# Two fp32 layers on one core: four small re-orderings around the adaLN sums, the gate products, v's transposes and the attention's denominators

## The chip, the cores and the metric

The kernel runs on one core of one Trainium2 chip. The metric is the device time of one execution in microseconds (us), lower is better. Engines: TensorE (PE; its weight loads are listed as PEld), VectorE (DVE), ScalarE (ACT), GpSimd (POOL) and SyncE (SP), whose queue starts most of the loads.

## The reference

A backbone of two layers over 256 latent and 256 context tokens, 1024 features, in float32:

```python
def modulate(x, shift, scale):
    return x * (1 + scale) + shift
def adaln(cvec, w, b):
    return jnp.split(jax.nn.silu(cvec) @ w + b, 6, axis=-1)
...
# every sub-layer: x <- LN(ALPHA*x + gate * F(x*(1+scale)+shift))
# layer 0: F = Conformer convolution module, then a squared-ReLU MLP
# layer 1: F = bidirectional chunkwise mLSTM (4 heads of 512, inner 2048), then the MLP
def sq_relu_mlp(u, w1, w2):
    return jnp.square(jax.nn.relu(u @ w1)) @ w2
...
q, k, v = xc @ w_q, xc @ w_k, xm @ w_v
gates = jnp.concatenate([q, k, v], axis=-1) @ w_gate + b_gate
...
den = jnp.sum(scores, axis=-1) + w_inter * jnp.einsum('bhtd,bhd->bht', qc, n)
h = num / jnp.maximum(jnp.abs(den), jnp.exp(-m_row))[..., None]
```

## The kernel before

Activations lie with features on the 128 partitions and tokens along the free axis; the two streams (latent, context) lie side by side, 512 columns. Every float32 operand is split into a rounded high part and a low part (`split`: ACT casts `wh`, DVE subtracts to get `wl`), and each product is three matmuls (`mm3`, L175, L178, L179; `mm3t`, L206 to L208, for products with the transposed result). Weights come in 1 MB loads (`raw_load`, L148, on SP's queue) into three buffers `raw`, and are split into four buffers `wh` and four `wl`. PSUM is shared by four kinds of bank: `mm` three, `ln` two, `cv` two, `fl` one.

The program is written in the order of its work, with generators that advance side work by one step between the pieces of a large product. The framework's scheduler sets each engine's order from the order of the program and from the semaphores that it needs; `issue_after(x)` asks that what is inside be put behind instruction x, and `lastmm[0]` is the newest large matmul. Each engine then runs its instructions in that order.

The places that the change touches:

- `AdaV` makes one adaLN vector on DVE beside a large product. `step()` loads a 256 KB piece of `ada_w` and adds it, times c, into accumulators (the tiles S and L). When a vector's pieces are through, two closures go onto the list `todo` and are run one at each later step: `sums` (four matmuls with a column of ones over the partitions, L431, and a copy into F on ACT, L433) and `end` (four transposes of F, L440, and an addition on DVE). `flush()` runs what is left. Three vectors are made: in the first MLP, in its second part, and in the mLSTM's products. The second is `ada_n1`, whose flush is in `feed0`, when the layer-norm of the first MLP is closed for the high half of the tokens. The first MLP's last product, w2 of part 3, goes over the high half of the tokens first and then the low half (`gemm2`); the epilogue L1043 adds each output to the residual x out of a `mm` bank, and the normalisation (L567, L568), the scaling (L590, ACT) and the subtraction (L591) of the high half run beside the low half's matmuls.
- `wgq_step` folds the gate's weights through wq, so that the gates can be had from the input: it loads a 1 MB piece of `wqT` and multiplies it with a 128x32 piece of the gate's weights, four matmuls of 512 columns at four column positions (L748), adding up in one `fl` bank over sixteen pieces. Behind the sixteenth, ACT copies the bank into F (L753) and four transposes (L756) turn it. `v_epi` ends each of the sixteen output tiles of v; `v_out` transposes the tile (L1193) and stores it, a tile later, through the list `late` and `flush()`. The loop over `gemm_steps(wv, ...)` (32 steps of 24 large matmuls) calls `wgq_step` in each of its first 16 steps and a step of the third AdaV in the other 16.
- `weights(h)` makes the attention's weights of head h: scores, exponentials, and on GpSimd (L1454) the sum `es` over the blocks. Two empty yields behind, it makes the denominators: `es` times a column of ones (L1461), Abs on ACT (L1463), two maxima with the guard and a reciprocal on DVE, in `rden[h]`. `attend(h)` makes the four outputs (direction by token block) in two `cv` banks, and DVE scales each by `rden` (L1533). ACT also runs the sigmoid of `gate_o` (L1500) and the exponentials (L1442) in that stretch, with a table load at each change between them. Generators of two heads run beside one another.

Of the kernel before, what the change touches and what calls it, by code (L numbers as in the profile page):

```python
# [14 lines left out]
P = 128  # L15
# [3 lines left out]
ET = E // P  # L19
# [51 lines left out]
def hybrid_kernel(ctx: ExitStack, tc: tile.TileContext, xT, vecs_d, wdw_d, ada0_w, ada_w, wg_d, pw1a, pw1, pw2, w1_0, w2_0,  # L71
                  w1_1, w2_1, up_x, up_z, wv, wo, bo_d, wk, wq, wqT, wdown, rows_d, out):
    nc = tc.nc
# [26 lines left out]
    def psum(tag="mm"):  # L100
        return pp.tile([P, 512], F32, tag=tag, name=nm(tag), bufs={"mm": 3, "ln": 2, "fl": 1, "cv": 2}[tag])
# [23 lines left out]
    ident = con.tile([P, P], F32, name="ident")  # L125
# [55 lines left out]
    lastmm = [None]  # L181
# [22 lines left out]
    def mm3t(ps, xh, xl, wh, wl, start, stop):  # L204

        nc.tensor.matmul(ps, xh, wh, start=start, stop=False)  # L206
        nc.tensor.matmul(ps, xl, wh, start=False, stop=False)  # L207
        nc.tensor.matmul(ps, xh, wl, start=False, stop=stop)  # L208
# [181 lines left out]
    class AdaV:  # L390
# [8 lines left out]
        def step(self):  # L399
            if self.todo:  # L400
                self.todo.pop(0)()
            n, kt = divmod(self.i, DT)
            if n == len(self.units):
                return
            if kt == 0:
                self.acc += [tmp("SL"[(len(self.acc) + i) // 2 % 2]) for i in range(len(self.streams))]
            w = adp.tile([P, 512], F32, tag="ar", name=nm("ar"))
            nc.sync.dma_start(w, ada_w[self.l, self.units[n], kt // 4, :, kt % 4 * 512:kt % 4 * 512 + 512])
            for i, s in enumerate(self.streams):
                a, c = self.acc[i - len(self.streams)], cs[:, kt, 14 + s:15 + s]  # L410
                if kt == 0:
                    o = nc.vector.tensor_scalar(a, w, c, None, op0=ALU.mult)
                    if i == 0:
                        tc.keep_in_program_order(o)
                else:
                    nc.vector.scalar_tensor_tensor(a, w, c, a, op0=ALU.mult, op1=ALU.add)  # L416
            self.i += 1
            if kt == DT - 1 and n < self.ncol and len(self.acc) == 4:
                accs, self.acc = self.acc, []
                u = self.units[n] + 1 - 4 // len(self.streams)  # L420
                self.todo += [lambda: self.sums(accs), lambda: self.end(u)]

        def flush(self):
            while self.todo:
                self.todo.pop(0)()
# [9 lines left out]
        def end(self, u):  # L435
            ns, s0 = len(self.streams), self.streams[0]
            nu, o = 4 // ns, _OFF[f"ada_b{self.l}"][0] + 4 * u
            tr = psum()
            for b in range(4):
                nc.tensor.transpose(tr[:, b * P:(b + 1) * P], self.sb[:, b * P:(b + 1) * P], ident)  # L440
            nc.vector.tensor_tensor(
                ada[self.l][:, 4 * u:4 * (u + nu), s0:s0 + ns].rearrange("p (v b) s -> p b v s", b=4),
                tr.rearrange("p (b v s r) -> p b v s r", b=4, v=nu, s=ns)[:, :, :, :, 0],
                vecs[:, o:o + 4 * nu].rearrange("p (v b o) -> p b v o", b=4, o=1).broadcast_to([P, 4, nu, ns]), op=ALU.add)
# [295 lines left out]
    def wgq_step():  # L740
        kt = len(wqs)
        if kt == 0:
            wqs.append(psum("fl"))
        else:
            wqs.append(None)
        raw = raw_load(wqT[kt])
        for j in range(4):
            nc.tensor.matmul(wqs[0][32 * j:32 * j + 32, :], wgp[0][:, kt, :], raw[:, j * 512:(j + 1) * 512],  # L748
                             start=kt == 0, stop=kt == ET - 1, tile_position=(0, 32 * j))
        if kt < ET - 1:  # L750
            return
        qsb = tmp("F")
        nc.scalar.copy(qsb, wqs[0])  # L753
        qtr = psum("fl")
        for b in range(4):
            nc.tensor.transpose(qtr[:, b * P:(b + 1) * P], qsb[:, b * P:(b + 1) * P], ident)  # L756
        nc.vector.tensor_copy(wgp[1].rearrange("p (j b) c -> p j b c", j=4)[:, :, :, 0:16],
                              qtr.rearrange("p (b j c) -> p j b c", b=4, j=4)[:, :, :, 0:16])
# [421 lines left out]
    def v_epi(m, ps):  # L1180
        vt = B("vt").rearrange("p a b -> p (a b)")[:, :T]
        nc.scalar.copy(vt, ps)
        vts.append(vt)
        flush()
        late.append(lambda: v_out(m, vt))

    def v_out(m, vt):
# [27 lines left out]
    vstep = 0  # L1215
    for _ in gemm_steps(wv, range(8), xm, T, v_epi):
        vstep += 1
        if vstep <= ET:
            wgq_step()
        else:  # L1220
            ada_n2.step()
        if vstep in (20, 26):
            xc_load(0 if vstep == 20 else 4)
# [196 lines left out]
    def weights(h):  # L1420


        es = ES()
        short = PW(F32R)
        for d in range(2):
            cidx = gcol(d, h)
            nb = psum("ln")
            nc.tensor.matmul(nb[:, :C], sel[d * 4 + h], negm, start=True, stop=True)
            yield
            for i, b in enumerate(blocks[d]):  # L1430
                q0, q1 = rng[d, b]
                if i != 1:
                    et = tmp("S")
                e_ = et[:, HI] if i == 1 else et[:, q0:q1]
                if b < 2:
                    nc.scalar.activation(e_, nb[:, q0:q1], AF.Exp, bias=acol[:, b, cidx:cidx + 1])
                else:
                    mk = mask[:, d, :, :].rearrange("p a t -> p (a t)")
                    off = {(0, 2): 0, (0, 3): 0, (1, 3): 0, (1, 2): P}[d, b]
                    nc.vector.scalar_tensor_tensor(e_, nb[:, q0:q1], acol[:, b, cidx:cidx + 1],  # L1440
                                                   mk[:, off:off + q1 - q0], op0=ALU.add, op1=ALU.add)
                    nc.scalar.activation(e_, e_, AF.Exp)  # L1442
                nc.vector.tensor_tensor(e_, e_, S[h, b][:, q0:q1], op=ALU.mult)
                if q1 - q0 == C:
                    t = PW(F32R)
                    hi, lo = t[:, LO], t[:, HI]
                else:
                    hi, lo = short[:, 2 * d * P:(2 * d + 1) * P], short[:, (2 * d + 1) * P:(2 * d + 2) * P]
                split(hi, lo, e_)
                pw[h, d, b] = (hi, lo)  # L1450
                if i == 1:
                    nc.gpsimd.tensor_tensor(es[:, d, :], et[:, LO], et[:, HI], op=ALU.add)
                elif i > 1:
                    nc.gpsimd.tensor_tensor(es[:, d, q0:q1], es[:, d, q0:q1], e_, op=ALU.add)  # L1454
                yield
        yield
        yield
        den = psum("ln")
        for d in range(2):
            for t in range(2):  # L1460
                nc.tensor.matmul(den[:, 2 * d + t:2 * d + t + 1], es[:, d, BLK[t]], ones[:, 0:1], start=True, stop=True)  # L1461
        rden[h] = rd = con.tile([P, 2, 2], F32, name=nm("rden"))
        nc.scalar.activation(rd, den[:, 0:4].rearrange("p (d t) -> p d t", d=2), AF.Abs)  # L1463
        for d in range(2):
            cidx = gcol(d, h)
            nc.vector.tensor_tensor(rd[:, d, :], rd[:, d, :], guard[:, :, cidx:cidx + 1].rearrange("p t o -> p (t o)"),
                                    op=ALU.max)
        nc.vector.reciprocal(rd, rd)


    xls = []
    for i in range(2):
        rx = raw_load(xl_dr[i].rearrange("p b c -> p (b c)"))
        for j in range(8):
            t = XL(F32R)
            split(t[:, LO], t[:, HI], rx[:, j * C:(j + 1) * C])
            xls.append((t[:, LO], t[:, HI]))
    og, yy, rden = {}, {}, {}

    def gate_o(h):  # L1480

# [32 lines left out]
    def attend(h):  # L1514
# [8 lines left out]
        for t in range(2):  # L1523
            for d in range(2):
                ps = psum("cv")
                bl = [b for b in blocks[d] if rng[d, b][0] <= t * P < rng[d, b][1]]
                for i, b in enumerate(bl):
                    hi, lo = pw[h, d, b]
                    sl = slice(t * P - rng[d, b][0], t * P - rng[d, b][0] + P)
                    vh, vl = [v_[:, (b % 2) * DH:(b % 2 + 1) * DH] for v_ in vs[b // 2]]  # L1530
                    mm3t(ps, hi[:, sl], lo[:, sl], vh, vl, i == 0, i == len(bl) - 1)
                o_ = og[h, d, t]
                nc.vector.scalar_tensor_tensor(o_, ps, rden[h][:, d, t:t + 1], o_, op0=ALU.mult, op1=ALU.mult)  # L1533
                yield
            hj = og[h, 0, t]
            nc.vector.tensor_tensor(hj, hj, og[h, 1, t], op=ALU.add)
            nc.vector.bn_stats(st_[:, t, :], hj)
            nc.vector.bn_aggr(mv[:, t, 0:2], st_[:, t, :])
            hs.append(hj)
            yield  # L1540
# [346 lines left out]
```

## Time and profile before

| what | value |
| --- | --- |
| three runs | median 1698.73 us (1697.41 to 1699.22) |
| the profiled execution | 1699.18 us; its span 1697.5 us |
| granted TensorE clock | 0.998 |
| instructions | 22796 |
| PE busy | 1669.2 us (98% of the span) |
| DVE, ACT, POOL busy | 1033.0, 744.0, 44.3 us |
| chain that ended last | PE 92%, DVE 5%, ACT 1%, DMA 1% |
| moved by DMA | 300.54 MB, 177 GB/s over the span |

In a row of the timeline stand start and duration in us, engine, line, operation, out<-in and the number of instructions joined (xcount); in square brackets the idle time of the engine ahead of it and what released it. A matmul's duration overlaps the next one's, so its cost is read from the starts. In the lists of waits stand total, times and longest, in us.

### The profile page before, as it was taken

Reading aid. Unit: us, or ns where it says so; the run is one execution under the profiler, and the core shown is the slowest. Engines: PE = TensorE matmul, PEld = TensorE weight load, DVE = VectorE, ACT = ScalarE, POOL = GpSimd, SP = SyncE. Lnnn points to the kernel's source line nnn. Section 1 sums busy time; section 2 is a strip of 40 time slices with the busy share of each in tenths; the row PEclk is TensorE's granted clock in tenths of the full one; section 3 lists DMA queues with packets and bytes.
Section 4 is the critical chain, followed back from the end, with each engine's and each line's share of the span. In section 5 each row is a group of like instructions: output and inputs, shape, how many; then the busy total and the mean of one; then the engine's idle time right before and its main releaser. Section 6 shows DMA issues by size and latency. Waiting matters only on the chain.

```text
span 1697.5 us, 22796 instructions
## 1 busy us (share of the span) xinstructions
PE 1669.2 (98%) x8878; PEld 1363.8 (80%) x8878; DVE 1033.0 (61%) x1841; ACT 744.0 (44%) x1195; POOL 44.3 (3%) x92
## 2 busy tenths in 40 slices
PE   7999999999999999999999999999999999999997
PEld 5655898878888998876788899888877878878886
DVE  5555795666645776751243653563487786776676
ACT  3312563232324476642333533442477564645443
POOL 0000000000000000000000000000011120000001
PEclk9999999999999999999999999999999999999999
DMA  8546322434424065567765752454454556756552
GB/s 340 198 156 243 111 75 95 157 128 146 145 100 148 2 211 180 183 238 252 251 214 174 251 181 105 155 189 171 157 190 176 193 195 209 257 211 229 192 184 89
DMA packets 70828, 300.54 MB, mean 177 GB/s; under 512 B 7170, under 2 KB 22018, under 8 KB 40384
## 3 DMA queue, kind: packets, MB, share of 16 engines
q1 hardware_dynamic: 53056, 284.39, 47.6%
q10 hardware_dynamic: 17664, 14.69, 2.7%
q8 instruction: 70, 1.15, 0.3%
q14 instruction: 38, 0.31, 0.1%
HBM read 283.32 MB, written 15.73 MB: 176 GB/s over the span
## 4 chain that ended last, share of the span: by engine, by line
PE 92%; DVE 5%; ACT 1%; issue 1%; DMA 1%; POOL 0%; SPq 0%; DVEq 0%; POOLq 0%; ACTq 0%
PE mm L175 17%; PE mm L178 17%; PE mm L179 17%; PE mm L190 7%; PE mm L191 4%; PE mm L206 3%; PE mm L207 3%; PE mm L208 3%; PE cv L208 2%; PE cv L207 2%; PE cv L206 2%; PE fl L335 1%; DVE wl L153 1%; PE fl L748 1%; PE cv L830 1%
## 5 line engine op out<-in xcount | busy, mean ns | idle before, releaser
L153 DVE TENSOR_TENSOR wl<-raw,wh 128x1024 fp32r<-128x1024 f32 x346 | 424.7, 1233 | 275.8 <-ACT wh L152 271.4
L152 ACT CAST wh<-raw 128x1024 fp32r<-128x1024 f32 x346 | 360.6, 1050 | 494.5 <-PE mm L178 269.0
L178 PE MATMUL mm<-u,wh 128*128 128x512 f32 (+1 forms) x808 | 292.9, 363 | 0.1
L175 PE MATMUL mm<-u,wh 128*128 128x512 f32 (+1 forms) x680 | 245.5, 361 | 0.2 <-ACT E L770 0.2
L179 PE MATMUL mm<-u,wl 128*128 128x512 f32 (+1 forms) x680 | 242.3, 357 | 0.0
L178 PEld LDWEIGHTS mm<-u,wh 128*128 128x128 f32 x808 | 153.4, 190 | 23.5 <-issue 1.8
L175 PEld LDWEIGHTS mm<-u,wh 128*128 128x128 f32 x680 | 129.2, 190 | 28.8 <-issue 9.1
L179 PEld LDWEIGHTS mm<-u,wl 128*128 128x128 f32 x680 | 129.2, 190 | 18.4 <-issue 0.2
L175 PE MATMUL mm<-xm,wh 128*128 128x512 f32 x256 | 102.2, 399 | 0.0
L206 PE MATMUL mm<-wh,xl 128*128 128x512 f32 x256 | 101.3, 396 | 0.5 <-ACT wh L152 0.5
L207 PE MATMUL mm<-wh,xl 128*128 128x512 f32 x256 | 100.9, 394 | 0.0
L179 PE MATMUL mm<-xm,wl 128*128 128x512 f32 x256 | 99.9, 390 | 0.0
L208 PE MATMUL mm<-wl,xl 128*128 128x512 f32 x256 | 99.6, 392 | 0.0
L175 PE MATMUL mm<-hid,wh 128*128 128x512 f32 (+1 forms) x256 | 93.1, 364 | 0.0
L178 PE MATMUL mm<-hid,wh 128*128 128x512 f32 (+1 forms) x256 | 92.8, 363 | 0.0
L179 PE MATMUL mm<-hid,wl 128*128 128x512 f32 (+1 forms) x256 | 92.7, 362 | 0.0
L190 PE MATMUL mm<-x,wh 128*128 128x512 f32 x232 | 81.0, 398 | 0.8 <-DVE x L1698 0.8
L416 DVE SCALAR_TENSOR_TENSOR S<-ar,cs,S 128x512 f32<-128x512 f32 x56 | 40.8, 749 | 61.3 <-DMA ar<-ada_w 61.0
L178 PE MATMUL mm<-qq,wh 128*128 128x272 f32 x256 | 73.9, 289 | 0.0
L175 PE MATMUL mm<-qq,wh 128*128 128x272 f32 x256 | 73.5, 289 | 0.0
L179 PE MATMUL mm<-qq,wl 128*128 128x272 f32 x256 | 73.5, 288 | 0.0
L190 PE MATMUL mm<-u,wh 128*128 128x512 f32 x192 | 68.6, 399 | 0.0
(507 smaller groups left out, 3277.8 us busy)
## 6 DMA issues: line engine op xcount, KB each, us to landing
raw<-w SPq DMA_DIRECT2D x64, 1024.0 KB, 4.8
raw<-wo SPq DMA_DIRECT2D x32, 1024.0 KB, 4.9
raw<-ada_w SPq DMA_DIRECT2D x26, 1024.0 KB, 5.9
ar<-ada_w SPq DMA_DIRECT2D x80, 256.0 KB, 3.4
raw<-wv SPq DMA_DIRECT2D x16, 1024.0 KB, 5.4
raw<-wqT SPq DMA_DIRECT2D x16, 1024.0 KB, 5.6
raw<-wq SPq DMA_DIRECT2D x16, 1024.0 KB, 4.9
raw<-wk SPq DMA_DIRECT2D x16, 1024.0 KB, 5.2
```

The costliest lines, as they stand in the source:

```text
L152: c = nc.scalar.copy(hi, src)
L153: nc.vector.tensor_tensor(lo, src, hi.bitcast(F32), op=ALU.subtract)
L175: a = nc.tensor.matmul(ps, wh, xh, start=start, stop=False)
L178: nc.tensor.matmul(ps, wh, xl, start=False, stop=False)
L179: lastmm[0] = nc.tensor.matmul(ps, wl, xh, start=False, stop=stop).ins
L190: todo = [lambda s_, e_: nc.tensor.matmul(ps, wh, r[0], start=s_, stop=e_), lambda s_, e_: nc.tensor.matmul(ps[:, :n], wl, r[0][:, :n], st ...
L191: lambda s_, e_: nc.tensor.matmul(ps[:, :n], wl, r[0][:, :n], start=s_, stop=e_)]
L206: nc.tensor.matmul(ps, xh, wh, start=start, stop=False)
L207: nc.tensor.matmul(ps, xl, wh, start=False, stop=False)
L208: nc.tensor.matmul(ps, xh, wl, start=False, stop=stop)
L335: a = nc.tensor.matmul(ps[32 * j:32 * j + 32], cs[:, kt, 14 - 2 * v:46 - 2 * v], blocks[kt], start=first and kt < 4, stop=last and kt >= 4 ...
L416: nc.vector.scalar_tensor_tensor(a, w, c, a, op0=ALU.mult, op1=ALU.add)
```

## The change

Four edits. The denominators move out of `weights(h)` into a function of their own, called in `attend(h)` behind the matmuls of the head's first output; odd heads sum `es` in the tile F. An AdaV's `sums` and `end` get an empty step between them, and the end's transposes are issued behind the newest large matmul. Two products of wq stand together at the odd steps 3 to 17 of v's product; the AdaV steps stay where they were. v's finished tiles are transposed two at a time.

```diff
@@ AdaV.step
-                self.todo += [lambda: self.sums(accs), lambda: self.end(u)]
+                self.todo += [lambda: self.sums(accs), lambda: None, lambda: self.end(u)]
@@ AdaV.end
             tr = psum()
-            for b in range(4):
-                nc.tensor.transpose(tr[:, b * P:(b + 1) * P], self.sb[:, b * P:(b + 1) * P], ident)
+            with tc.issue_after(lastmm[0]):
+                for b in range(4):
+                    nc.tensor.transpose(tr[:, b * P:(b + 1) * P], self.sb[:, b * P:(b + 1) * P], ident)
@@ v_epi
         vts.append(vt)
-        flush()
+        if m % 2 == 0:
+            flush()
         late.append(lambda: v_out(m, vt))
@@ loop over gemm_steps(wv, ...)
         vstep += 1
-        if vstep <= ET:
+        if vstep % 2 and 3 <= vstep <= ET + 1:
             wgq_step()
-        else:
+            wgq_step()
+        if vstep > ET:
             ada_n2.step()
@@ weights(h)
-        es = ES()
+        es = tmp("F").rearrange("p (d t) -> p d t", d=2) if h % 2 else ES()
...
-        yield
-        yield
-        den = psum("ln")
+        sums[h] = es
+
+    def denominators(h):
+
+        den, es = psum("ln"), sums[h]
         for d in range(2):
             for t in range(2):
                 nc.tensor.matmul(den[:, 2 * d + t:2 * d + t + 1], es[:, d, BLK[t]], ones[:, 0:1], start=True, stop=True)
...
@@ attend(h), behind an output's matmuls
                     mm3t(ps, hi[:, sl], lo[:, sl], vh, vl, i == 0, i == len(bl) - 1)
+                if h not in rden:
+                    denominators(h)
                 o_ = og[h, d, t]
```

Lines after the change are one higher from L421 on, three to six higher in the last third.

On PE in v's product, before: one tile's transposes and one product, two steps (48 large matmuls) from the next transposes; `fl` is the bank of the products.

```order
L179 MATMUL mm_7189<-xm_6683,wl_7307 128x512
L1193 MATMUL ln_7336<-ident,vt_7290 128x128 x4
L748 MATMUL fl_6737<-raw_7344,wgq_556 32x512 x4
L175 MATMUL mm_7358<-xm_5920,wh_7362 128x512
L178 MATMUL mm_7358<-u_5921,wh_7362 128x512
```

The same place after, at the last pair of products; L757 is the transposing of the folded gate weights.

```order
L179 MATMUL mm_7330<-xm_6275,wl_7335 128x512
L749 MATMUL fl_6797<-raw_7362,wgq_556 32x512 x4
L749 MATMUL fl_6797<-raw_7368,wgq_556 32x512 x4
L175 MATMUL mm_7331<-xm_5920,wh_7386 128x512
L178 MATMUL mm_7331<-u_5921,wh_7386 128x512
L179 MATMUL mm_7331<-xm_5920,wl_7387 128x512
L175 MATMUL mm_7331<-xm_5969,wh_7386 128x512
L757 MATMUL fl_7376<-ident,F_7374 128x128 x4
```

Two products stand directly behind one another; the transposes that need ACT's copy F stand four large matmuls behind them, where there were twelve.

On DVE at the close of the first MLP, before: x_119 to x_417 are features of the high half in normalisation, `mm_5000` the low half's second output.

```order
L556 TENSOR_TENSOR L_4896<-ident,lc_4893 128x512
L567 TENSOR_TENSOR x_119<-x_119,ln_4898 128x256
L568 TENSOR_TENSOR x_119<-x_119,ln_4898 128x256
L567 TENSOR_TENSOR x_153<-x_153,ln_4898 128x256
L1043 SCALAR_TENSOR_TENSOR x_325<-mm_5000,ada_105,x_325 128x256
L568 TENSOR_TENSOR x_153<-x_153,ln_4898 128x256
```

The same place after, the end of the normalisation; ahead of it stand now the addition of `ada_106` and the six operations that make the columns `ca` and `cb`.

```order
L569 TENSOR_TENSOR x_371<-x_371,ln_4892 128x256
L568 TENSOR_TENSOR x_417<-x_417,ln_4892 128x256
L592 TENSOR_TENSOR u_4951<-S_4952,u_4950 128x256
L569 TENSOR_TENSOR x_417<-x_417,ln_4892 128x256
L1044 SCALAR_TENSOR_TENSOR x_325<-mm_5000,ada_105,x_325 128x256
L592 TENSOR_TENSOR u_4959<-S_4960,u_4958 128x256
```

The emptying of the bank `mm_5000` moved from behind the third normalisation operation to behind the sixteenth.

On PE in head 0's attention, before: the denominators among the products of `gate_o`.

```order
L207 MATMUL mm_11047<-wh_11135,xl_10760 128x512
L1461 MATMUL ln_11083<-ones,es_10911 128x1
L208 MATMUL mm_11047<-wl_11136,xl_10760 128x512
L1461 MATMUL ln_11083<-ones,es_10911 128x1
L206 MATMUL mm_11048<-wh_11135,xl_10757 128x512
```

After: one block behind the first output, `cv_11301`; `cv_11322` is the second, `cv_11373` the third.

```order
L208 MATMUL cv_11301<-wl_11280,pw_10949 128x512
L1466 MATMUL ln_11311<-ones,es_10911 128x1 x4
L206 MATMUL cv_11322<-wh_11275,pw_10999 128x512
L207 MATMUL cv_11322<-wh_11275,pw_10999 128x512
L208 MATMUL cv_11322<-wl_11276,pw_10999 128x512
```

The block stands 16 large matmuls ahead of the third output's first one.

More of the change, by code (lines that the diff above doesn't have):

```diff
@@ L1477, in hybrid_kernel @@
             xls.append((t[:, LO], t[:, HI]))
-    og, yy, rden = {}, {}, {}
+    og, yy, rden, sums = {}, {}, {}, {}
     def gate_o(h):
```

## The prediction

> **What bounds the kernel now.** I read the page's head, its engine table and the shares of the chain first, then the waits of PE, then the timeline of PE at each place that the diff touches.
>
> ```profile
> span 1697.5 us, 22796 instructions
> PE 1669.2 (98%) x8878; PEld 1363.8 (80%) x8878; DVE 1033.0 (61%) x1841; ACT 744.0 (44%) x1195; POOL 44.3 (3%) x92
> PE 92%; DVE 5%; ACT 1%; issue 1%; DMA 1%; POOL 0%; SPq 0%; DVEq 0%; POOLq 0%; ACTq 0%
> ```
>
> The tensor engine is busy for 98% of the span and is 92% of the chain that ended last. So an edit counts in full where it shortens PE's own stream or one of PE's waits; what it does to DVE, ACT or the queues counts only when PE then stands still. The large matmuls are untouched, and what can be won is what lies between them. From the waits of PE (total, times, longest, in us), the three lines that the change touches:
>
> ```profile
> PE ln L1461 <- POOL es L1454: 1.6, 3, 0.9
> PE mm L440 <- ACT F L433: 0.8, 1, 0.8
> PE mm L206 <- ACT wh L152: 0.5, 1, 0.5
> ```
>
> That is 2.9 us in all, 0.2% of the span. The rest of a possible gain is the price of interrupting the stream of 128x512 matmuls. About 0.2% (3.4 us) is what a measurement of this kernel can tell from no change.
>
> **Part 1, the products of wq two by two.** Sixteen products of wgq (8 matmul records each) stand alone in the stream today. The timeline of PE around one of them (start, duration, instruction):
>
> ```profile
> 736.73 0.39 PE L179 MATMUL mm<-xm,wl 128*128 128x512 f32 x1
> 737.05 1.06 PE L748 MATMUL fl<-raw,wgq 128*32 128x512 f32 x8
> 738.05 0.50 PE L175 MATMUL mm<-xm,wh 128*128 128x512 f32 x1
> 738.38 0.39 PE L178 MATMUL mm<-u,wh 128*128 128x512 f32 x1
> 738.62 0.39 PE L179 MATMUL mm<-xm,wl 128*128 128x512 f32 x1
> ```
>
> The large matmuls start 0.23 us apart (738.38 to 738.62 here; 0.227 on a long stretch). From 736.73 to 738.62 are three such steps, 0.68 us; it took 1.89. The product costs 1.21 us: 1.00 from its start to the next matmul, the rest in going in and out of the stream. The changed kernel issues 16 records in one piece, eight times. No such piece of wgq is in the trace, but the same form with 16 records is, in the third adaLN vector:
>
> ```profile
> 1529.37 0.39 PE L190 MATMUL mm<-x,wh 128*128 128x512 f32 x1
> 1529.69 1.92 PE L335 MATMUL fl<-raw,cs 128*32 128x512 f32 x16
> 1531.55 0.50 PE L206 MATMUL ln<-wh,hid 128*128 128x512 f32 x1
> 1531.89 0.40 PE L207 MATMUL ln<-wh,hid 128*128 128x512 f32 x1
> 1532.13 0.40 PE L208 MATMUL ln<-wl,hid 128*128 128x512 f32 x1
> ```
>
> From 1529.37 to 1532.13 are 2.76 us, less 0.68 is 2.08. Two single products cost 2.42, a double one 2.08: 0.34 saved, eight times, **-2.7 us**. Bounds: nothing saved, and 0.68 saved each (the second product entering for the 0.8 us by which eight more records lengthen the row and no more), so 0 to -5.4. I take the middle because it is measured on the same form.
>
> What hangs on it: each pair needs two 1 MB loads of wqT at once, and their two buffers become free only behind the pair. That is a rival below. The transposes behind the last product wait for one ACT copy with 4 matmuls (0.9 us) for cover where there were 12; the copy itself lasts 0.6, so I cost that at 0, and at up to 1 us if ACT is in the middle of a cast.
>
> **Part 2, v's transposes two tiles at once.** Sixteen blocks of four:
>
> ```profile
> L1193 PE MATMUL ln<-ident,vt 128*128 128x128 f32 x64 | 9.8, 276 | 0.0
> ```
>
> In the new order four of the eight pairs of blocks stand directly behind one another and four have 4 large matmuls between them, because the second transposes wait for the second copy. If a merged block saves the same share as a wgq pair, 0.34 of 2.42 (14%), then of the four blocks' worth, at most 9.8 us / 16 = 0.61 each, it is 4 x 2 x 0.61 x 0.14 = 0.7; but going out and in is less than that for short blocks. I take **-0.2 us**, 0 to -0.7.
>
> **Part 3, adaLN sums a step apart.** The timeline of PE at the first vector's end, and the row of the second's:
>
> ```profile
> 376.68 0.39 PE L179 MATMUL mm<-hid,wl 128*128 128x512 f32 x1
> 377.45 0.60 PE L431 MATMUL mm<-S,ones 128*32 128x512 f32 x2
> 378.82 0.66 PE L440 MATMUL mm<-ident,F 128*128 128x128 f32 x4 [0.76 <-ACT F L433]
> 379.23 0.48 PE L175 MATMUL mm<-hid,wh 128*128 128x512 f32 x1
> 511.14 0.60 PE L440 MATMUL mm<-ident,F 128*128 128x128 f32 x4
> ```
>
> From 376.99 on the four sums run, ACT copies them, and the four transposes stand directly behind and wait 0.76 us. With an empty step between and the transposes issued behind the newest large matmul, 25 rows lie between: the wait goes, **-0.7 us**. The second end (511.14) and the third wait for nothing now, so there is nothing to gain there.
>
> The second one is moved to a worse place. Its vector has 32 steps and 34 calls; the empty step pushes the end past the last call, into the flush when the last layer-norm of the high half is closed. Then its transposes stand behind the last output of that half, and on DVE one addition and six small operations that make the scale and shift columns stand inside the normalisation. The rows of that place, from the timelines of DVE, ACT and PE:
>
> ```profile
> 575.28 0.42 DVE L567 TENSOR_TENSOR x<-x,ln 128x256 f32<-128x256 f32 x1 [1.28 <-PE ln L561]
> 576.47 0.48 DVE L1043 SCALAR_TENSOR_TENSOR x<-mm,ada,x 128x256 f32<-128x256 f32 x1
> 576.19 0.60 ACT L590 ACTIVATE u<-x,cb,ca 128x256 fp32r<-128x256 f32 x1 [3.57 <-DVE x L568]
> 577.32 0.60 ACT L590 ACTIVATE u<-x,cb,ca 128x256 fp32r<-128x256 f32 x1
> 582.03 0.28 PE L175 MATMUL mm<-hid,wh 128*128 128x256 f32 x1
> ```
>
> The operation at 576.47 empties the PSUM bank of the low half's second output, and the fifth output, which begins on PE at 582.03, writes that bank. Today it stands behind three normalisation operations and is 5 us early. In the new order it stands behind all sixteen and six subtractions. The subtractions wait for ACT's pairs of scalings, 1.13 us apart (576.19 to 577.32). With the transposes (0.47 us) and the seven operations ahead, I put the first scaling at about 576.8; the sixth pair ends near 576.8 + 6 x 1.13 = 583.6, the subtraction and the normalisation behind it and the bank's operation (0.42 + 0.42 + 0.48, overlapping a little) end near 584.6. PE, later by the transposes, wants the bank at 582.5. Cost **+2.0 us**. Bounds: if DVE and ACT run as tightly as 0.34 us an operation, +0.5; if they run at DVE's present mixed pace of 25 us for 61 operations (0.41), 22 x 0.41 = 9.0 from 575.9, +2.9 with the bank's operation:
>
> ```profile
> 575.00:600.00 25.00, 25.00 (x208) 24.81 (x207) 23.68 (x61) 15.93 (x29) 0.00 (x0) 1.00 0.12 43
> ```
>
> **Part 4, the denominators.** Today 32 short matmuls (16 pairs in ones, twos and fours) are spread over the gaps and can come before GpSimd has finished the sums es. Behind the change they come in four blocks of eight records, behind the head's first output, long after es.
>
> ```profile
> L1461 PE MATMUL ln<-ones,es 128*128 128x1 f32 x32 | 4.6, 240 | 1.7 <-POOL es L1454 1.6
> 1285.97 0.39 PE L206 MATMUL mm<-wh,xl 128*128 128x512 f32 x1
> 1286.95 0.60 PE L1461 MATMUL ln<-ones,es 128*128 128x1 f32 x4 [0.60 <-POOL es L1454]
> ```
>
> The number of matmuls is the same, so their own time stays. What goes is the waits: from 1285.97 to 1286.95 is 0.98 where 0.23 is the pace, so 0.75 lost where the list prints 0.60; the 1.6 us of the list are 2.0 by that ratio. With the 0.5 of the wait for a cast behind the last denominator (ACT's queue had held the cast behind its wait), it is -2.5.
>
> That odd heads sum into the tile F costs nothing: its last user before them is the third adaLN vector's end, a stage before the heads.
>
> New is that the first output's scaling, and behind it the third output (two cv banks), waits for Abs on ACT, two maxima and a reciprocal on DVE. In head 0, ACT reloads its tables at that time:
>
> ```profile
> 1283.02 1.28 ACT L1442 ACT_TABLE_LOAD   x1
> 1284.32 0.31 ACT L1442 ACTIVATE S<-S 128x128 f32<-128x128 f32 x1
> L1533 DVE SCALAR_TENSOR_TENSOR og<-cv,rden,og x16: 736/750/751, 1280.7 to 1472.2; 128x512 f32<-128x512 f32 x16
> L1463 ACT ACTIVATE rden<-ln x4: 173/174/174, 1270.1 to 1385.6; 128x4 f32<-128x4 f32 x4
> ```
>
> ACT leaves its last table load and exponential at 1284.6; Abs, 0.17, stands behind them, then two maxima of 0.15, the reciprocal of 0.17 and the scaling of 0.75, 1.4 us, with some 0.1 for each hand-over: 1286.4. The end of the first output is near 1282.1 in today's time, some 0.8 earlier without the blocks that stood ahead of it; the third output begins 0.9 (the new block) and 16 matmuls (3.6) later, 1285.8. That is +0.6 there; a cast of the next weights stands behind Abs too and is wanted 4 matmuls earlier. Heads 1 and 2 have room (24 matmuls and more, no table load), head 3 perhaps 0.1. New wait **+0.7**, bounds 0 and +2. Together **-1.8 us**, bounds -2.9 and -0.5.
>
> [...]
>
> **The sum.** -2.7 - 0.2 - 0.7 + 2.0 - 1.8 = -3.4 us. The profiled execution took 1699.18 us (span 1697.5 and 1.7 around it), so 1695.8 by its time; the median of the three runs, 1698.73, is 0.45 lower, which gives **1695.3 us**. It is a forecast of many small terms whose largest two have opposite signs.
>
> **The rivals.**
>
> *The merges bring nothing.* If the cost of a product is its 8 records and not the way in and out, -2.7 and -0.2 fall to about -0.3. Against it stands the 16-record row with 2.08; for it, that this row is followed by another kind of matmul (wh stationary), which may hide some. Then 1695.8 + 2.6 - 0.45 = 1697.9: within 0.2%.
>
> *The flush and the denominators cost more.* If the bank's wait takes its upper bound, +2.9, and head 0's wait +2, the sum is -3.4 + 0.9 + 1.3 = -1.2: 1697.5, within 0.2% as well. What speaks for it: DVE is already 95% busy in those 25 us (23.68 of 25.00).
>
> *Slower: the pairs wait for their loads.* The stage's loads, from the DMA view and the waits of SP's queue, 730 to 850 us:
>
> ```profile
> DMA packets 9462, 30.54 MB, mean 254 GB/s; under 512 B 759, under 2 KB 5321, under 8 KB 6345
> raw<-wqT SPq DMA_DIRECT2D x14, 1024.0 KB, 5.4
> raw<-wv SPq DMA_DIRECT2D x10, 1024.0 KB, 5.4
> SPq L148 <- PE fl L748: 77.5, 15, 7.8
> ```
>
> Three buffers hold raw weights. Today one load of wqT is asked for every 6.7 us; behind the change two are asked for together, when the pair is through, and the next pair is 48 x 0.227 = 10.9 us behind its end. In that time two loads of wqT and one of wv, 3.15 MB, have to land. At the mean rate of 254 GB/s they take 12.4 us, 1.5 too many; that is where it decides: above 3.15 MB / 10.9 us = 289 GB/s nothing waits. Seven pairs have a pair ahead of them: 7 x 1.5 = 10.5 us, so 1695.3 + 10.5 = 1705.8, slower. What speaks against it: 77.5 us of SP's time went on waiting for the products to free a buffer, so the mean rate is what was asked for and not what the memory gives; two loads of 5.4 us one behind the other take 10.8, and wv's is split into its halves well ahead of use. [...]
>
> *It doesn't do what it says.* The order of PE's rows shows every one of the four edits made, so this has no chance of its own.
>
> **How the numbers follow.** Forecast 0.58, merges without gain 0.12, flush and denominators dearer 0.14, loads late 0.10; 0.06 is left for a larger gain than I see (up to -5.4 for the pairs, -2.9 for the denominators: 1691). The forecast's own range is 1692.5 to 1698, from its terms' bounds taken two at a time. The range for 8 in 10 is 1691.5 to 1700.5: it holds the two cases near 1697.5 and some of a small lateness of loads, and leaves out the full one. "Faster by over 0.2%" begins at 1695.3, the middle of the forecast: 0.29 of its 0.58, 0.06 of the larger gain, and the forecast's tail towards a cheaper flush, which I hold for somewhat likelier than a dearer one because 2.0 was taken with ACT's whole pace, 0.08: **0.43**. Slower by over 0.2% is 0.10 for the loads and 0.04 for two mishaps at once: **0.14**. The rest, **0.43**, is within 0.2%.
>
> **What would show it.** Right: 16-record rows of wgq with about 2.1 us from the matmul ahead to the third behind, and no idle time noted beside them; no wait of L441 for F; no wait of ones,es; one idle time of 1.5 to 2.5 us near 584 us on PE, released by DVE x. Wrong: idle time beside raw<-wqT from DMA (the loads); a wait of cv on DVE og over 1.5 us (denominators); PE running through 582 to 585 without a gap (the flush costs nothing, and the total is near 1693); a double product at 2.4.

## The result and the profile after

The changed kernel takes 1695.8 us (median of 20 runs, 1692.83 to 1698.71), the kernel before 1698.25 (20 runs beside them): ratio 0.9985, 95% interval 0.9979 to 0.9990, 2.5 us less. In a second set of 12 runs it was 1694.61 against 1698.45, ratio 0.9977 (0.9967 to 0.9987). One run of the kernel before took 4330 us and is left out of all figures. The gain is real: 0.15% in the first set, inside the 0.2% that the prediction took for no change, and 0.23% in the second. The first median is 0.5 us from the forecast (1695.3). But the runs of the changed kernel lie 6 to 8 us apart, and the experiments had to say why.

The head of the page and the waits of PE after the change (total, times, longest, in us):

```profile
span 1695.9 us, 22802 instructions
PE 1668.2 (98%) x8878; PEld 1367.8 (81%) x8878; DVE 1031.1 (61%) x1841; ACT 743.0 (44%) x1195; POOL 44.3 (3%) x92
PE mm L175 <- DVE x L1044: 1.1, 1, 1.1
PE fl L206 <- DVE E L1604: 1.0, 2, 0.6
PE mm L208 <- DVE wl L153: 0.6, 1, 0.6
```

All three waits of PE that the prediction listed (for es, for F, for a cast) are gone. Three others stand in their place, 2.7 us in all where it was 2.9. The gain is in PE's stream and not in its waits. From the timeline of PE, a pair of products, whose cost is read as before, from the start of the matmul ahead to the third behind:

```profile
747.38 0.39 PE L179 MATMUL mm<-xm,wl 128*128 128x512 f32 x1
747.69 1.92 PE L749 MATMUL fl<-raw,wgq 128*32 128x512 f32 x16
749.55 0.50 PE L175 MATMUL mm<-xm,wh 128*128 128x512 f32 x1
749.89 0.40 PE L178 MATMUL mm<-u,wh 128*128 128x512 f32 x1
750.13 0.40 PE L179 MATMUL mm<-xm,wl 128*128 128x512 f32 x1
```

From 747.38 to 750.13 are 2.75 us, less three steps of 0.227 is 2.07; the row of the same form in the trace of before had given 2.08. Then the flush, first DVE (start of the normalisation, and the emptying of the bank), then PE:

```profile
573.69 0.42 DVE L568 TENSOR_TENSOR x<-x,ln 128x256 f32<-128x256 f32 x1 [1.28 <-PE ln L562]
581.39 0.47 DVE L1044 SCALAR_TENSOR_TENSOR x<-mm,ada,x 128x256 f32<-128x256 f32 x1
```

```profile
580.56 0.28 PE L179 MATMUL mm<-hid,u 128*128 128x256 f32 x1
581.92 0.39 PE L175 MATMUL mm<-hid,wh 128*128 128x256 f32 x1 [1.08 <-DVE x L1044]
```

PE stops ahead of the matmul that the prediction named, for 1.24 us more than the usual step of 0.12; the sign named beforehand was 1.5 to 2.5. And one thing that no part of the change explains: PE at half pace, at the start of the attention.

```profile
1247.05 0.70 PE L1431 MATMUL ln<-negm,ident 36*128 36x256 f32 x2
1247.68 0.63 PE L208 MATMUL mm<-wl,xl 128*128 128x512 f32 x1
1248.11 0.63 PE L206 MATMUL mm<-wh,xl 128*128 128x512 f32 x1
...
1250.67 0.63 PE L206 MATMUL mm<-wh,xl 128*128 128x512 f32 x1
1251.42 0.39 PE L208 MATMUL mm<-wl,xl 128*128 128x512 f32 x1
```

The matmuls start 0.43 us apart for 3.4 us and then 0.23 again, which costs some 1.3 to 1.6 us here (table below). It happens once more from 1503.89 to 1507.30. The profiled run of before has neither of these two stretches, but it has one at 170 us, and so have six others of the twelve profiled runs (e8 has it at 108). The granted clock (the figure behind the last count in brackets) of these stretches, first before, then after:

```profile
170.24:173.65 3.41, 3.41 (x17) 3.19 (x16) 1.19 (x3) 3.13 (x9) 0.00 (x0) 0.50 0.70 293
```

```profile
1247.90:1251.30 3.40, 3.40 (x9) 2.61 (x9) 1.45 (x4) 3.37 (x7) 0.73 (x1) 0.50 0.88 281
1503.89:1507.29 3.40, 3.40 (x11) 2.92 (x12) 3.36 (x15) 3.40 (x11) 0.00 (x0) 0.50 0.99 407
```

To keep such things apart, I compare six stretches of each profiled run with the same stretches of before. The marks are starts on PE: the first adaLN sums, the first transposes behind the first MLP (128x128 into cv), the last product cv<-vt,wgv, the transposes of negm ahead of the attention, the second transposes of res behind it, and the end of the span. In the trace of before they are at 376.99, 642.65, 937.55, 1248.71, 1500.66 and 1697.5 us. Differences to before in us; "h" marks a half-pace stretch in the columns "attention" and "tail".

| kernel | to the first sums | MLP | v | to the attention | attention | tail | span |
| --- | --- | --- | --- | --- | --- | --- | --- |
| changed kernel | -0.65 | +0.43 | -2.80 | -0.02 | +0.03 h | +1.41 h | -1.6 |
| the same again (e10) | +0.26 | +0.41 | -2.74 | -0.22 | -0.12 h | +1.41 h | -1.0 |
| pairs alone (e1) | -1.93 | 0.00 | -2.54 | +0.19 | -0.13 | +0.21 | -4.2 |
| adaLN alone (e2) | -1.83 | +0.40 | -0.01 | 0.00 | +1.40 h | -0.06 | -0.1 |
| denominators alone (e3) | -1.72 | -0.03 | +0.01 | -0.19 | -1.55 | -0.02 | -3.5 |
| end before the flush (e4) | -1.54 | -0.74 | -2.43 | -0.06 | -1.49 | -0.04 | -6.3 |
| the same again (e8) | +0.32 | -0.75 | -2.61 | -0.16 | -0.15 h | +1.35 h | -2.0 |
| e4, v one by one (e6) | -0.99 | -0.73 | -2.53 | -0.12 | +0.11 h | +1.36 h | -2.9 |
| e4, three products (e5) | -1.77 | -0.73 | +7.58 | -0.13 | -1.68 | +0.13 | +3.4 |
| e4, gap filled, ten (e7) | -0.44 | -0.74 | -2.98 | -0.12 | -1.65 | +0.73 | -5.2 |
| e4, gap filled, five (e9) | -0.28 | -0.74 | -2.97 | +0.20 | -1.68 | -0.03 | -5.5 |

The first column is the same work in every kernel, and it differs by 2.3 us between runs: single spans are not to be compared, stretches are. An early half-pace stretch (at 170 or 108 us) is probably part of it: the four runs without one (e1, e2, e4, e6) are among the six shortest there, and the six longest all have one.

### The profile page after: what moved, and what is told of

Same layout as the page of the kernel before. It is cut to its first block, busy times and chain, and to the rows that moved or that the text cites. A ratio compares the mean times of both kernels' runs of the same rounds, so it can differ in the third digit from the quotient of the medians.

```text
span 1695.9 us, 22802 instructions
## 1 busy us (share of the span) xinstructions
PE 1668.2 (98%) x8878; PEld 1367.8 (81%) x8878; DVE 1031.1 (61%) x1841; ACT 743.0 (44%) x1195; POOL 44.3 (3%) x92
## 5 line engine op out<-in xcount | busy, mean ns | idle before, releaser
L175 PE MATMUL mm<-u,wh 128*128 128x512 f32 (+1 forms) x680 | 244.7, 360 | 0.3 <-ACT E L771 0.3
L175 PEld LDWEIGHTS mm<-u,wh 128*128 128x128 f32 x680 | 129.2, 190 | 28.7 <-issue 9.1
L175 PE MATMUL mm<-xm,wh 128*128 128x512 f32 x256 | 101.0, 395 | 0.0
L175 PE MATMUL mm<-hid,wh 128*128 128x512 f32 (+1 forms) x256 | 93.3, 364 | 1.1 <-DVE x L1044 1.1
L175 PE MATMUL mm<-qq,wh 128*128 128x272 f32 x256 | 73.5, 288 | 0.0
## 6 DMA issues: line engine op xcount, KB each, us to landing
ar<-ada_w SPq DMA_DIRECT2D x80, 256.0 KB, 3.4
```

The costliest lines, as they stand in the source:

```text
L175: a = nc.tensor.matmul(ps, wh, xh, start=start, stop=False)
```

## The experiments

### e1: only the pairs

The edit is the loop over `gemm_steps(wv, ...)` of the change and nothing else.

> Only the products of wq two by two, all else as before. Theory (each pair saves the way in and out of the stream once, 0.34 us): pieces of 16 records with 2.09 us each instead of two of 1.22, so 8 x 0.34 = 2.7 us less at equal clock, 1698.3 to about 1695.6; no idle time beside the loads of wqT. Rival (a pair's two loads are late): idle time on PE from DMA raw<-wqT ahead of some pairs, and less than 2 us saved.

Measured: 1697.08 us (11 runs), ratio 0.9994 (0.9985 to 1.0003), which can't be told from no change. The stage of v is 2.54 us shorter, with pieces of 16 records at 2.08 to 2.09 and no wait for a load. So the theory holds for the stage, and the total shows only half of it; the runs reach from 1694.5 to 1699.4.

### e2: only the adaLN edit

The edit is the empty step in `step` and the `issue_after` in `end`.

> Only the adaLN sums a step apart and the end's transposes behind the newest large matmul. Theory: the wait of 0.76 at the first end goes (-0.74), and the second end in the flush brings one idle time of about 1.1 to 1.3 us on PE near 583 us, released by DVE's emptying of a bank; together +0.3 to +0.6 us. Rival (the stop near 583 comes from the changed phase of other edits, not from this one): no idle time there, and 0.7 us less than before.

Measured: 1699.49 us (11 runs), ratio 1.0010 (1.0001 to 1.0019): a little slower. From the timeline of PE:

```profile
579.36 0.28 PE L179 MATMUL mm<-hid,u 128*128 128x256 f32 x1
580.72 0.38 PE L175 MATMUL mm<-hid,wh 128*128 128x256 f32 x1 [1.08 <-DVE x L1044]
```

The stop comes with this edit alone. The MLP's stretch is 0.40 longer: -0.73 up to the second sums, +1.13 behind them. This run also has a half-pace stretch near 1249 us, with the attention as it was before the change.

### e3: only the denominators

The edit moves them out of `weights` into `denominators(h)`, with the sums of odd heads in F.

> Only the denominators behind each head's first output. Theory: no wait of PE for es (-1.6 and the ways in and out around it, about 3 in all), new waits of 0.6 us in head 0 (for wl behind the denominators' operations on DVE) and 0.4 to 1.0 in head 2: together 1.0 to 2.0 us less at equal clock. Rival (the denominators' place makes PE's clock fall at the start of the attention, as in the trace of the changed kernel): a stretch of 3.4 us at half pace near 1248 us in this trace too and a mean clock lower than that of the kernel before, so no gain.

Measured: 1697.13 us (11 runs), ratio 0.9992 (0.9983 to 1.0001), which by its interval can't be told from no change either. The attention is 1.55 us shorter. It has no half-pace stretch, and, what weighs more against the rival, e2 has one with the denominators in their old place. From the waits of PE:

```profile
PE fl L206 <- DVE E L1602: 1.0, 2, 0.6
PE mm L208 <- DVE wl L153: 0.6, 1, 0.6
```

The two new waits are those of the changed kernel, and neither is the wait for Abs that the prediction named. The wait for wl has the size that was expected for e3, but not the cause: it ends at 1276.83 us in e3, and the denominators begin only behind it, at 1279.01.

### e4 and e8: the end before the flush

```diff
-                self.todo += [lambda: self.sums(accs), lambda: None, lambda: self.end(u)]
+                gap = [lambda: None] if n + 1 < len(self.units) else []
+                self.todo += [lambda: self.sums(accs), *gap, lambda: self.end(u)]
```

> The whole change, but without the empty step for a vector's last unit, so that the second end stays inside its 34 steps and out of the flush. Theory: the idle time of 1.08 us near 581 us goes and nothing takes its place; 1.2 us less than the changed kernel at equal clock, 1694.6. Rival (DVE is late there in any case, being busy for 95% of that stretch): the idle time stays or moves a few us, and the time is that of the changed kernel, 1695.8.

> The fourth kernel once more, beside the three others on the same chip. Theory: 1694.3 us again, within 0.7; the trace again without a stop near 581 us. Rival (its gain was the chance of where half-pace stretches fell): about 1695.8.

Measured: 1694.26 us, ratio 0.9975 (0.9966 to 0.9984), and again 1693.69, ratio 0.9977 (0.9968 to 0.9986), 11 runs each. From the timeline of PE in e4, behind an unbroken row of matmuls, the one that stopped before:

```profile
579.75 0.28 PE L175 MATMUL mm<-hid,wh 128*128 128x256 f32 x1
```

It has no bracket. The MLP is 0.74 us shorter than before, as the first end alone gives, and 1.2 shorter than in the changed kernel. The median of the 22 runs is 1694.1, that of the changed kernel's 32 is 1694.9: the direction and the stretch are shown, the difference of the totals is within what these runs scatter. The two profiled runs of this one kernel are the clearest pair of the study: 1692.99 us without any half-pace stretch, 1697.23 with these two, and with a third at 108 us in a start that is 1.9 us longer.

### e5: three products together

```diff
-        if vstep % 2 and 3 <= vstep <= ET + 1:
-            wgq_step()
-            wgq_step()
+        if vstep % 3 == 0 and vstep <= ET + 2:
+            for _ in range(3 if vstep < ET else 1):
+                wgq_step()
```

> The fourth kernel (second end before the flush) with three products of wq together at every third step, all three buffers of raw weights at once, instead of two. Theory (two by two leaves the loads time; only the way in and out is saved): three by three must go wrong, since a triple's loads and v's own weights pass the same three buffers: idle time of PE of 2 us or more behind most triples, from DMA raw or from the casts behind it, 5 to 15 us slower than the fourth kernel. Rival (loads never matter here, there is room for any grouping): pieces of 24 records save another 0.2 us a product, 0.7 us less in all, no idle time.

Measured: 1703.21 us (6 runs), ratio 1.0031 (1.0019 to 1.0042), 9 us over e4. From the timelines of PE and of ACT:

```profile
772.19 0.76 PE L175 MATMUL mm<-xm,wh 128*128 128x512 f32 x1 [2.34 <-ACT wh L152]
819.08 0.50 PE L175 MATMUL mm<-xm,wh 128*128 128x512 f32 x1 [2.55 <-ACT wh L152]
```

```profile
771.10 1.99 ACT L152 CAST wh<-raw 128x1024 fp32r<-128x1024 f32 x2 [1.55 <-DMA raw<-wv]
```

v's own weights come late because the triple holds all three buffers: SP starts their loads at 766.19 and 812.87 us, 1.1 us into a triple (765.06 and 811.74). It happens twice and not behind most triples, 5.1 us of waits with a third, smaller one; the matmuls behind both stops run at half pace for some 3 us (behind the first they start 0.43 us apart up to 775.44), and about 2 us of the stage's 10 I can't place. So here the loads do limit how many products may stand together: at three PE waited 5.1 us for the casts behind them, at two (e1) there was no wait for a load.

### e6: v's transposes one by one

The edit puts `flush()` back into every `v_epi`, in e4.

> The fourth kernel with v's tiles transposed one at a time, as before the change. Theory: two at once saves nothing that shows (0 to 0.3 us over the stage of v); the stage from the first MLP to v's last product is within 0.3 us of the fourth kernel's. Rival: each joined pair saves the way in and out of the stream, 0.2 us and more, 1 us in all, and this kernel is 1 us slower.

Measured: 1694.28 us (10 runs), ratio 0.9977 (0.9968 to 0.9986). The stage of v is -2.53, against -2.43 and -2.61 of e4 and e8, within 0.3 as expected. But two things cancel there. From the first to the last matmul of L175 on xm in v's product are 200.86 us in e1 and e6, with tiles transposed one by one, and 200.42 in e7 and e9, with two at a time and the same products of wq: joining saves 0.44 us. In the four other kernels with joined tiles the transposes of the folded gate weights begin 0.15 to 0.48 us late, and the way is longer by about as much (200.62 to 200.96). From the timelines of ACT and PE in e4:

```profile
841.20 2.00 ACT L152 CAST wh<-raw 128x1024 fp32r<-128x1024 f32 x2 [5.59 <-DMA raw<-wv]
843.10 0.57 ACT L755 COPY F<-fl 128x512 f32<-128x512 f32 x1
```

```profile
843.73 0.66 PE L758 MATMUL fl<-ident,F 128*128 128x128 f32 x4 [0.31 <-ACT F L755]
```

ACT's copy stands behind a cast whose load came in late, the case that the prediction had priced at up to 1 us. Over the six traces with joined tiles 0.2 us of the gain is left on average.

### e7 and e9: work of no use in a gap

Ten, or five, 128x128 matmuls into a bank that the next transposes overwrite, ahead of the gap near 1497 us, in e4:

```diff
     ada_unit()
+    tr0 = psum("ln")
+    for _ in range(10):
+        nc.tensor.matmul(tr0[:, :P], ident, ident, start=True, stop=True)
     with tc.issue_after(scaled):
-        ln1(turn(1, 0), 1, 0)
+        ln1(turn(1, 0, tr=tr0), 1, 0)
```

> The fourth kernel with ten extra 128x128 matmuls of no use on PE in the idle time of 1.32 us near 1497 us. Theory (a stretch of 3.4 us at half pace follows when PE has done little for some us, and comes or goes with the moment of the run): the extra work costs nothing, no such stretch follows this gap, and the mean clock of the runs rises by up to 0.0005, the median falls by 0 to 0.7 us. Rival (the half pace has another cause, or the extra matmuls count as little): clock and time spread as in the fourth kernel, or the gap grows by what the extra matmuls take.

> The fourth kernel with five extra 128x128 matmuls in the gap near 1497 us, half as many as before, to fit the idle 1.32 us. Theory: the delay of 0.7 us that ten caused is gone, the stretch at half pace behind the gap stays away, so the median is 0.4 to 0.7 us below the fourth kernel's 1694.1 (22 runs) and its runs spread less. Rival: five don't keep the clock up; clock and spread as in the fourth kernel.

Measured: with ten, 1694.12 us (9 runs, 1692.56 to 1695.04), ratio 0.9975 (0.9966 to 0.9985), mean clock of the runs 0.9979 where e4 and e8 have 0.9971; with five, 1693.12 (5 runs, 1691.53 to 1694.55), ratio 0.9966 (0.9954 to 0.9978), clock 0.9970. The timelines of PE, of e7 and of e9:

```profile
1497.69 2.27 PE L1720 MATMUL ln<-ident 128*128 128x128 f32 x18
1499.80 1.04 PE L1690 MATMUL ln<-ident,res 128*128 128x128 f32 x8
```

```profile
1498.16 1.16 PE L1720 MATMUL ln<-ident 128*128 128x128 f32 x8
1499.45 1.18 PE L1690 MATMUL ln<-ident,res 128*128 128x128 f32 x8
```

Ten last 2.1 us and delay the tail by 0.73; five fit. In neither profile does a half-pace stretch follow, and e8's highest runs are missing. That agrees with the theory and doesn't prove it: there are 14 runs, the mean clock rose in e7 only, and e1 has no stretch behind this gap either, with nothing filled in and at nearly the same place in the raster on which the stretches lie (described below; a line lies 5.8 us behind the second transposes of res in e1 and e9, 6.0 in e7). e9 has the lowest median of the study; its lead over e4 is within the scatter.

### e10: the change once more

> The changed kernel once more, beside the kernel before on the same chip. Theory (its stages are 3.7 us shorter and half-pace stretches, which come by chance at two places, give 1 to 1.5 of that back on average): median 1695.5 to 1696.2, ratio 0.9985, mean clock near 0.997, runs at the highest clock below 1694.5. Rival (the stretches are tied to this kernel's order, always two): a narrow spread near 1697.5.

Measured: 1694.61 us, below the expected 1695.5 to 1696.2. Eight of the twelve runs have a mean clock of 0.998 and lie from 1691.95 to 1694.70, four have 0.995 or 0.996 and lie from 1696.99 to 1700.21. So the stretches come and go in one kernel, against the rival. Its profiled run is one with both (1236 to 1256 and 1490 to 1512 us; the figure behind the last count in brackets is PE's clock):

```profile
1236.00:1256.00 20.00, 19.35 (x82) 14.43 (x80) 14.60 (x33) 13.76 (x20) 2.26 (x3) 0.91 0.49 171
1490.00:1512.00 22.00, 19.41 (x102) 15.01 (x101) 19.23 (x48) 11.26 (x30) 0.00 (x0) 0.92 0.64 235
```

## Why the prediction was right, term by term

**Products two by two, forecast -2.7.** Held: -2.54 alone, and the price of a double product (2.07 to 2.09) is that of the row it was taken from (2.08). The rival that merges bring nothing fell with it. The rival of the loads fell at two and was met at three. The case for it rested on a mean rate of 254 GB/s, and 289 was to decide. Beside and behind a pair of the changed kernel the rate (last figure) is above that:

```profile
747.00:758.00 11.00, 11.00 (x57) 7.70 (x56) 4.51 (x6) 3.96 (x7) 0.00 (x0) 1.00 0.93 340
```

So the mean was what was asked for. The trace of before has a stretch of 11 us at such a rate too, outside the rows that the prediction shows: 365 GB/s from 152 to 163 us.

**v's transposes, -0.2.** Held within its bounds: -0.44 for the joining, and 0 to +0.5 for ACT's late copy (e6).

**The first end, -0.7, and the flush, +2.0.** The first gave -0.73. The stop in the flush is at its place, behind its cause, but 1.24 us where 2.0 was put. By the second sums the run lay 1.4 us ahead of before's (503.18 for 504.56). Taken back by that, the working had the normalisation start at 574.5, the bank's operation end at 583.2 and PE want the bank at 581.1. Measured are 573.7, 581.9 (581.39 and 0.47) and 580.7. So the start was put 0.8 us too late, since I had let the transposes and the seven small operations delay it, and they fell into DVE's waits for PE; the pace was 0.5 too slow (8.2 us from start to end, not 8.7); PE's own earlier arrival takes 0.4 back. DVE and ACT ran nearly as tightly as the lower bound had it. That bound was added up wrongly: by the sum of the upper one, 575.9 + 22 x 0.34 + 0.48 - 582.5, it is +1.4 and not +0.5. With the bank so much earlier, the whole edit cost 0.40 where 1.3 was forecast.

**The denominators, -1.8.** Measured -1.55, but out of other terms, and that they add up to nearly the forecast is luck. The run to read is e3, which has no half-pace stretch in the attention. It lies 1.93 us ahead of before's there (1246.78 for 1248.71), and its times are given below with that added. The wait for Abs behind the table loads never came (rows of e3 on ACT, DVE and PE):

```profile
1279.69 1.28 ACT L1442 ACT_TABLE_LOAD   x1
1281.20 0.16 ACT L1465 ACTIVATE rden<-ln 128x4 f32<-128x4 f32 x1
1282.08 0.75 DVE L1537 SCALAR_TENSOR_TENSOR og<-cv,rden,og 128x512 f32<-128x512 f32 x1
1279.01 0.95 PE L1463 MATMUL ln<-ones,es 128*128 128x1 f32 x8
1283.59 0.39 PE L206 MATMUL cv<-wh,pw 128*128 128x512 f32 x1
```

The third output starts at 1285.5 in before's time, near the 1285.8 that was worked out. The first scaling ends at 1284.8, 0.8 us ahead of it, where 1286.4 was worked out. The step that failed is that PE was moved to its new time and ACT was left at its old one: ACT's last table load starts at 1281.6 and not at 1283.0. Before the change ACT had stood still in front of head 0's Abs, which waited for PE's denominators:

```profile
1270.06 0.17 ACT L1463 ACTIVATE rden<-ln 128x4 f32<-128x4 f32 x1 [1.57 <-PE ln L1461]
```

That Abs no longer stands there, and PE, which releases ACT's casts (the one at 1274.00 us before, behind 0.46 us of idle time), is itself earlier; how much of the 1.4 us each of the two gives is not shown. Two other terms were off as well, and the bound of -2.9 doesn't follow from its terms, which give -2.5 with no new wait. Read from the starts of the large matmuls around them, the denominators took 6.6 us in ten places and take 3.6 in four blocks: 3.0 less, where 2.0 was taken for the waits and nothing for the ways in and out of the stream. And other waits came, 2.1 us by the same reading where 0.7 was put: one for wl at 1276.83 (0.8), ahead of the block, into which PE ran because the denominators no longer held it, and two for the bank `fl` in head 2 (0.75 and 0.5, released by DVE's E). With the wait for a cast gone (0.6), the terms are -3.0 + 2.1 - 0.6 = -1.5.

**The sum.** -0.73 + 1.13 - 2.8 - 1.55 is about -3.9 by stretches, where -3.4 was forecast. The medians moved by 2.5 and 3.8. What lies between are the start's 2.3 us of scatter and the half-pace stretches, which the prediction didn't have at all. So the mechanism held for the products, the first end and the flush; that the first median came out 0.5 us from the forecast is in part luck, since the flush cost less than was put and the stretches took some of the gain back.

**The half-pace stretches.** In each profiled run the starts and ends of these stretches lie whole multiples of 3.413 us apart (after the change they start at 169.28, 1247.89 and 1503.89 us: 316 and 75 times 3.4133; before, one starts at 170.24, and the half clock at the end of the span at 1692.58: 446 times). So I lay a raster of that width over each trace, and a stretch begins at one of its lines. Where the raster lies differs from run to run, and in these traces whether a stretch follows a quiet place goes with it. After the change the lines at 1247.89 and 1503.89 lie 2.2 us behind the start of negm's transposes (1245.67) and 6.2 behind the second transposes of res (1497.65); before, lines lie 0.1 and 3.6 us behind the one (1248.71) and 0.8, 4.2 and 7.6 behind the other (1500.66), and no stretch follows. In the five runs with a stretch near 1247 us a line lies 2.0 to 2.4 us behind the start of negm's transposes; in the seven without one it lies at most 1.7 or more than 3.2 us behind. In the four with a stretch near 1504 a line lies 6.2 to 6.5 us behind the second transposes of res; in the eight without, none lies between 6.1 and 7.1.

In all four the two stretches are 256.0 us apart, 75 widths. With a first stretch, the second transposes of res come 252.0 us behind those of negm in the changed kernel (1245.67 to 1497.65), and 75 widths on from the first stretch a line lies just where it brings the second. With the attention of before they come 253.4 us behind (e2, 1247.27 to 1500.62); the line then lies 4.7 us behind res, and e2 has no second stretch. By this working the shorter attention brings a second stretch to the runs that have the first. It rests on four traces and one, and no run tried it.

The mean clocks of the runs fit in part: 0.996 or lower in 10 of 32 runs of the changed kernel and in 2 of 74 of the kernel before, but in none of the 11 of e3, which has the shorter attention too. The averages are 0.99706 and 0.99754, a difference of 0.0005 or 0.8 us. They are a rough measure: in every trace the clock is at half for the last 3.8 to 7.0 us too (4.9 before, 4.2 after), when PE has nothing left to do, and between the shortest and the longest of these the mean differs by about as much as a stretch moves it (0.001).

## What to carry to other kernels

Small matmuls of one form that stood alone between large ones cost a way in and out of the stream here (1.21 us for one product of wq, 2.07 to 2.09 for two together), and the price of joining them could be read beforehand from a longer row of the same form (2.08). Before an empty step is added to a list of deferred work, count the steps that are left: here the last entry fell into the flush that closes the list, its operations stood ahead of the normalisation's on DVE, and PE stopped for 1.24 us. Where an edit moves one engine earlier, move the engines that wait for it too before working out what is late (ACT's last table load came 1.4 us before the time at which the working had left it). For effects of a thousandth, compare stretches between the same marks of two traces; the totals here carry 2.3 us of scatter of the start, and half-pace stretches of 1.3 to 1.6 us each.

## What the runs showed of the hardware

PE's granted clock was 0.50 for 3.41 us at a time: from 170.24 to 173.65 us before, and from 1247.89 to 1251.30 and from 1503.89 to 1507.30 after, where it was 1.00 between those two. In the later part of the kernel such stretches were seen behind two places: behind 0.65 us of idle time and matmuls over 36 rows (near 1247 us), and behind idle times of 0.51, 1.32 and 0.77 us with small matmuls and transposes between them (near 1504 us). A stretch costs some 1.3 to 1.6 us there, is seen in 5 of the 12 profiled runs (in four of them at both places), and comes in some runs of a kernel and not in others (e8 has both, e4, the same kernel, neither); in e5 it follows both stops of 2.3 and 2.6 us. The starts and ends within a trace lie whole multiples of 3.413 us apart (316 and 75 between the three starts after the change), and in these traces whether a stretch follows one of the two places goes with where that place lies in this raster. What sets the raster, and what makes the clock fall, no run shows.

DMA moved 340 GB/s for 11 us beside v's product in the changed kernel (747 to 758 us), while its mean from 730 to 850 us was 254 before: there the mean was set by what was asked for.
